# Clearing the substitution's result tiles and the HGRN queries' tiles on ScalarE in place of GpSimd

## The chip, the cores and the metric

The kernel runs on one core of a Trainium2 chip. The time is device microseconds (us) of one execution on that core. Its engines are called as in the profile: PE is TensorE, DVE is VectorE, ACT is ScalarE, POOL is GpSimd, SP is SyncE, which mostly issues DMAs. POOL issues DMAs of its own, too. Each engine runs its instructions in one fixed order and waits, by semaphores, for what other engines and DMAs deliver.

## What is computed

Two layers of a hybrid backbone for 512 latent tokens and a prefix of 256 context tokens, model width 1024, all in float32. Cut to what matters:

```python
for l in range(2):
    hl, hc = modulate(rmsnorm(xl), ...), modulate(rmsnorm(xc), ...)   # adaLN from c and c_ctx
    pl, pc = split_in(hl @ w_in[l]), split_in(hc @ w_in[l])           # one input projection
    dn = deltanet_group(...)   # gated delta rule, 4 heads of 64, chunks of 64, both directions
    sw = swa_group(...)        # 8 query heads, 2 kv heads, window 128, a sink, plus the context
    hg = hgrn2_group(...)      # HGRN2, 4 heads of 64, chunks of 64, both directions
    x = x + gate * (concat(dn, sw, hg) @ w_out[l])
    x = x + gate * (square(relu(modulate(rmsnorm(x)) @ w_ff1[l])) @ w_ff2[l])   # width 4096
return rmsnorm(xl)             # the context's stream is needed up to layer 1's projections
```

Two places of it bear on the change. The delta rule solves, for each chunk, a unit lower triangular system (`triangular_solve(a, rhs, unit_diagonal=True)`). The HGRN group forms masked products of queries and keys within a chunk.

## The kernel before, in words

**Products.** A float32 weight piece is split in two: L540 (ACT) casts it to `hi`, L541 (DVE) makes `lo`, and three matmuls, L554, L555 and L556, go over each tile of 128 rows. That is most of PE's work: input and output projections and the MLP, with L600 for the modulation vectors (adaLN).

**Stages of a layer.** The input projection fills tiles in SBUF and spills some of them to DRAM (`hq`, `hf`, `hi` for HGRN; `dg`, `hg` for the gates, L851). Then three groups run side by side. (1) Delta: `delta_prep` builds the chunk matrices (L1017 to L1041); `delta_inverse` calls `delta_blocks` for the substitution. That inverts blocks of 32 rows on DVE, in 31 pairs of a product (L1104) and an addition (L1105) of changing length; the result tile is `Yb`, cleared at L1092 with a diagonal of ones put in at L1093. Its blocks go through DRAM (`xu`, L1113, L1116, L1118) and are combined by small matmuls (L1135, L1139). `delta_chain` walks the chunks (L1177 to L1220) and `delta_norm` normalises (L1243 to L1257). (2) Attention: scores (L1450), softmax (L1475 and L1476 on DVE, L1480 and L1483 on ACT), products with the values (L1503, L1512). (3) HGRN: loads of `hf` and `hi` (L1273, L1282), two query tiles `qb`, cleared at L1299, of which the first then receives the queries by L1301; the second gets them times the forget products by L1315. Only the two blocks that belong to a head are written, the rest of the tile has to be zero, since L1309 and L1329 multiply the whole. Then the levels (L1329 and on), the chain of chunks (L1352 to L1395), and `head_norm` (L864 to L886). The output projection reads the three results (`yd`, `ys`, `yh`).

**What sets the order.** Each stage is a Python generator. `run(...)` (L274) advances several of them in turns, and `ahead(g, n)` gives the instructions of one a priority. A scheduler (`tile.TileContext(..., schedule_with_timeline_sim=True)`) then fixes the order of each engine from its own estimates of how long each instruction takes; so another engine for one instruction can change the order of many. In layer 0 the context's chain and HGRN run first (some 300 to 500 us), in layer 1 the three groups of the latent run together:

```python
run(self.ahead(delta(), 3000), self.ahead(att(), 1000), hg())
```

Here `att()` ends with the output projection's share of the attention (`ys`), whose products can stand between the steps of the other two.

**Memory.** SBUF is cut by hand: an arena and three regions r1, r2 and r3. Buffers are reused, so a clear waits for the last reader of what was there before. A tile of zeros of 128x256 exists (`self.zero`, L481, cleared once by DVE).

**Clears.** There are ten: `Yb` four times (64x1024 for the context, 128x1024 for the latent, in two layers) and the two `qb` three times (128x1024 for the context of layer 0, 128x2048 for the latent of either layer; the context of layer 1 needs no queries).

Of the kernel before, what the change touches and what calls it, by code (L numbers as in the profile page):

```python
# [167 lines left out]
def bc(ap, axis, n):  # L168
    ap = ap.unsqueeze(axis)
    return ap.broadcast_to(list(ap.shape[:axis]) + [n] + list(ap.shape[axis + 1:]))  # L170
# [99 lines left out]
def h4(ap):  # L270
    return ap.rearrange("p (h i) -> p h i", i=64)
# [33 lines left out]
class Net:  # L305
# [74 lines left out]
    def setup(self):  # L380
        nc = self.nc
# [66 lines left out]
        for l in range(DEPTH):  # L448
            if l:
                nc.vector.tensor_tensor(out=cum, in0=cum, in1=lb[:, :, :, l], op=ALU.add)  # L450
            v = self.lbn[:, l]
# [25 lines left out]
        st = self.keep(768)  # L477
        self.sd = st[:, 512:768]
        self.sh = st[:, 0:256].rearrange("p (a i) -> p a i", a=4)
        self.zero = st[:, 256:512].rearrange("p (a i) -> p a i", a=4)  # L480
        nc.vector.memset(self.zero, 0.0)  # L481
        kv = self.keep(2048)
        self.kT = kv[:, 0:1024]
        self.vS = kv[:, 1024:2048].rearrange("p (b c) -> p b c", b=8)
# [2 lines left out]
        self.ctx.kv0, self.lat.kv0 = 0, 512  # L487
        self.wh = Ring(self.wmem, 2, 1024)
        self.wl = Ring(self.wmem, 2, 1024)


    def x_load(self, seg, queue=None):
# [585 lines left out]
    def delta_blocks(self, seg):  # L1078
        nc, Uv = self.nc, seg.U
        n, u = 2 * seg.nc, slice(seg.u0, seg.u0 + 2 * seg.nc)  # L1080
        half, size = slice(4 * n, 8 * n), slice(0, 8 * n)
        Pb, Qb, Yb, tb = self.get(1024), self.get(1024), self.get(1024), self.get(256)
        P, Q, Y = (b.v.rearrange("p (a b) -> p a b", a=32) for b in (Pb, Qb, Yb))

        def quarters():

            for i in range(8):
                fw, hf, jb = i < 4, i // 2 % 2, i % 2
                rows = slice(64 * hf + 32 * jb, 64 * hf + 32 * jb + 32)
                yield slice(i * n, i * n + n), hf if fw else 1 - hf, rows, slice(32 * jb, 32 * jb + 32), fw, fw == (jb == 0)  # L1090

        nc.gpsimd.memset(Yb.v[size], 0.0)  # L1092
        nc.gpsimd.memset(Yb.v[size, 0:1024:33], 1.0)  # L1093

        nc.gpsimd.dma_start(out=seg.ud[:], in_=Uv[:, :, u])
        for blk, vv, rows, cols, fw, first in quarters():
            nc.gpsimd.dma_start(out=(P if fw else Q)[blk], in_=seg.ud[rows, vv, :, cols].rearrange("r u i -> u r i"))
        yield 8.0

        nc.vector.tensor_copy(P[half], Q[half].rearrange("p a b -> p b a"))  # L1100
        for c in range(31):
            m = 31 - c
            t = tb.v[size, :(c + 1) * m].rearrange("p (r m) -> p r m", m=m)
            nc.vector.tensor_tensor(out=t, in0=bc(Y[size, :c + 1, c], 2, m), in1=bc(P[size, c, c + 1:], 1, c + 1), op=ALU.mult)  # L1104
            nc.vector.tensor_tensor(out=Y[size, :c + 1, c + 1:], in0=Y[size, :c + 1, c + 1:], in1=t, op=ALU.subtract)  # L1105
            yield 0.3 + (c + 1) * m / 480
        Pb.free()
        tb.free()
        Z, Bb = Q, self.get(2 * n * 32)
        B = Bb.v.rearrange("p (v u i) -> p v u i", v=2, u=n)  # L1110
        nc.vector.tensor_copy(Z[size], Y[size].rearrange("p a b -> p b a"))
        for i, b in enumerate((Yb, Qb)):
            nc.gpsimd.dma_start(out=seg.xd[i], in_=b.v[size].rearrange("p (a b) -> p a b", a=32))  # L1113

        for blk, vv, rows, cols, fw, first in quarters():
            nc.gpsimd.dma_start(out=Uv[rows, vv, u, cols], in_=seg.xd[0 if fw else 1, blk].rearrange("u r i -> r u i"))  # L1116
            if first:
                nc.gpsimd.dma_start(out=B[rows, vv], in_=seg.xd[1 if fw else 0, blk].rearrange("u r i -> r u i"))  # L1118
        yield 10.0
        Qb.free()  # L1120
        Yb.free()
        Hr = Ring(self, 2, 512)
        for vv in range(2):
            firsts = []
            for hf in range(2):
                a, b = 64 * hf, 64 * hf + 32
                sa, sb = slice(0, 32), slice(32, 64)
                if hf != vv:
                    a, b, sa, sb = b, a, sb, sa
                firsts.append((slice(a, a + 32), slice(b, b + 32), sa, sb))  # L1130
            ph, pu, H = self.bank("ni"), self.bank("ni"), Hr()
            U = Uv[:, vv, u]
            for ra, rb, sa, sb in firsts:
                for k in range(n):
                    nc.tensor.matmul(ph[rb, k * 32:k * 32 + 32], lhsT=U[ra, k, sb], rhs=B[ra, vv, k], start=True, stop=True)  # L1135
                nc.scalar.copy(H[rb, :n * 32], ph[rb, :n * 32])
            for ra, rb, sa, sb in firsts:
                for k in range(n):
                    nc.tensor.matmul(pu[ra, k * 32:k * 32 + 32], lhsT=H[rb, k * 32:k * 32 + 32], rhs=U[rb, k, sb], start=True, stop=True)  # L1139
                nc.scalar.activation(out=U[ra, :, sb], in_=pu[ra, :n * 32].rearrange("p (u i) -> p u i", i=32), func=AF.Copy, scale=-1.0)  # L1140
            yield 2.0
        Bb.free()
        Hr.free()
# [123 lines left out]
    def hgrn(self, l, seg, need):  # L1267
        nc, T, nb, nC, r = self.nc, seg.T, seg.nb, seg.nc, seg.r
# [3 lines left out]
        for d in range(2):  # L1272
            nc.gpsimd.dma_start(out=kk[d], in_=seg.spill[l][d])  # L1273
            for p in range(2):
                a, na, b = (w[:, l, d, p:p + 1] for w in (self.lba, self.lbn, self.lbb))
# [5 lines left out]
        v = vb.v.rearrange("p (b c) -> p b c", b=nb)  # L1281
# [4 lines left out]
        def cells():  # L1286

            for n in range(2 * nb):
                for g in range(2):
                    t0 = n % nb * 128 + g * 64  # L1290
                    yield n, heads[g], n // nb, n // nb * nC + n % nb * 2 + g, slice(t0, t0 + 64)

        if need:

            qb = [self.get(4 * T) for _ in range(2)]
            qq = [b.v.rearrange("p (e x i) -> p e x i", e=2, i=64) for b in qb]
            qf = [[b.v[rows, e * 2 * T:e * 2 * T + 2 * T] for e, rows in enumerate(heads)] for b in qb]
            for b in qb:
                nc.gpsimd.memset(b.v, 0.0)  # L1299
            for e, rows in enumerate(heads):  # L1300
                nc.gpsimd.dma_start(out=qf[0][e].rearrange("p (a t) -> p a t", a=2), in_=seg.spill[l][2][rows])  # L1301

            scb = self.get(nb * 256)
            sc = scb.v.rearrange("p (n e i) -> p n e i", e=2, i=64)
            nc.vector.tensor_tensor(out=ks, in0=kk[0], in1=kk[1], op=ALU.add)
            for n, g, p, x, t in cells():
                if n % 4 == 0 and g is heads[0]:
                    ps = self.bank("hg")
                nc.tensor.matmul(ps[g, n % 4 * 128:n % 4 * 128 + 128], lhsT=ks[:, p, t], rhs=qq[0][:, :, x], start=True, stop=True)  # L1309
                if n % 4 == 3 and g is heads[1]:  # L1310
                    nc.vector.tensor_tensor(out=scb.v[:, (n - 3) * 128:(n + 1) * 128].rearrange("p (n i) -> p n i", i=64), in0=h4(ps),
                                            in1=bc(self.c["hd"], 1, 8), op=ALU.mult)
            for d in (1, 0):
                for e, rows in enumerate(heads):
                    nc.vector.tensor_tensor(out=qf[d][e], in0=qf[0][e], in1=F[d][rows].rearrange("p a t -> p (a t)"), op=ALU.mult)  # L1315
            yield T / 60
# [29 lines left out]
        for d in range(2):  # L1346
            for b0 in range(0, nb, 2):
                pt = self.bank("hg")
                for b in (b0, b0 + 1):
                    for p in range(2):  # L1350
                        c = (b - b0) * 256 + p * 128
# [24 lines left out]
        if need:  # L1376
# [13 lines left out]
            for c in range(nC):  # L1390
                g, b = c % 2, c // 2
# [364 lines left out]
```

## Time and profile before

| | |
|---|---|
| median of 3 runs | 2086.23 us (2084.28 to 2090.1) |
| profiled execution | 2089.67 us |
| span of its profile | 2087.8 us |
| mean granted clock of PE | 0.964 |
| PE busy | 1975.2 us (95%) |
| DVE busy | 1225.9 us (59%) |
| ACT busy | 860.6 us (41%) |
| POOL busy | 149.0 us (7%) |

Busy time is what an engine spends in instructions, its DMA issues, branches and semaphore waits aside. Matmuls overlap, so a busy PE is not a PE at its peak. The chain is followed back from the last instruction, at each step to what released it. Granted clock is the share of the full TensorE clock that the throttle gave, here 1.0 or about half. The profile's records are in the line numbers of the kernel before.

### The profile page before, as it was taken

What the parts mean: (1) busy time and instruction counts of PE and PEld (TensorE: products, weight loads), DVE (VectorE), ACT (ScalarE), POOL (GpSimd) and SP (SyncE); (2) the same over time, 40 slices, a digit from 0 to 9 for tenths busy, and PEclk for the clock granted to TensorE, in tenths of its full rate; (3) what the DMA queues carried; (4) which work ended last, traced back from release to release, by engine and by line L of the source; (5) the groups of instructions that cost most, each with busy time, mean ns of one, the idle gap of its engine ahead of it and who ended that gap; (6) DMA issues with size and microseconds to landing.
All of it is one profiled execution on the core that took longest, in us unless ns stands there. A gap on an engine that the chain in (4) does not pass through costs nothing.

```text
span 2087.8 us, 38082 instructions
## 1 busy us (share of the span) xinstructions
PE 1975.2 (95%) x15506; PEld 1627.2 (78%) x15506; DVE 1225.9 (59%) x2794; ACT 860.6 (41%) x1707; POOL 149.0 (7%) x289
## 2 busy tenths in 40 slices
PE   5999999899899999799999998999899979999996
PEld 3777888779899997788788875767678857888885
DVE  5675873756976676766333334756787573333335
ACT  3432354245556563452524232325544434334241
POOL 0001242000000000011000000012300000000000
PEclk9998997999999999899999999999989989999998
DMA  8545342165333342343222245364300222222222
GB/s 321 167 133 168 104 137 86 43 205 169 106 118 102 113 141 82 115 133 109 92 101 84 99 154 168 123 205 141 110 12 3 82 71 101 91 101 92 98 85 80
DMA packets 72831, 242.46 MB, mean 116 GB/s; under 512 B 10320, under 2 KB 13520, under 8 KB 72528
## 3 DMA queue, kind: packets, MB, share of 16 engines
q1 hardware_dynamic: 58608, 199.45, 28.4%
q0 software_dynamic: 12176, 35.19, 5.2%
q10 hardware_dynamic: 1872, 5.38, 0.8%
q8 instruction: 122, 2.00, 0.4%
q14 instruction: 53, 0.43, 0.1%
HBM read 218.21 MB, written 19.14 MB: 114 GB/s over the span
## 4 chain that ended last, share of the span: by engine, by line
PE 66%; issue 22%; DVE 5%; DMA 4%; ACT 2%; POOL 0%; SPq 0%; POOLq 0%; ACTq 0%; DVEq 0%
PE psum L554 15%; PE psum L556 15%; PE psum L555 14%; PE psum L600 3%; PE psum L1512 2%; PE psum L1503 2%; PE psum L1450 2%; DMA arena<-in_ada 1%; DMA r<-in_ada 1%; PE psum L1177 1%; PE psum L1329 1%; PE psum L1135 1%; PE psum L572 1%; PE psum L574 1%; PE psum L1139 1%
## 5 line engine op out<-in xcount | busy, mean ns | idle before, releaser
L554 PE MATMUL psum<-r,weights 128*128 128x512 f32 (+1 forms) x2288 | 823.9, 361 | 10.7 <-ACT arena L782 3.3
L556 PE MATMUL psum<-r,weights 128*128 128x512 f32 (+1 forms) x2288 | 819.8, 359 | 0.6 <-DVE weights L541 0.6
L555 PE MATMUL psum<-r,weights 128*128 128x512 f32 (+1 forms) x2288 | 818.7, 358 | 0.6 <-DVE r L1532 0.3
L540 ACT CAST weights<-arena 128x1024 fp32r<-128x1024 f32 (+3 forms) x295 | 293.6, 996 | 666.2 <-PE psum L555 583.7
L554 PEld LDWEIGHTS psum<-r,weights 128*128 128x128 f32 x2288 | 432.9, 189 | 96.1 <-issue 13.3
L541 DVE TENSOR_TENSOR weights<-arena,weights 128x1024 fp32r<-128x1024 f32 (+3 forms) x295 | 341.0, 1156 | 281.2 <-ACT weights L540 265.0
L556 PEld LDWEIGHTS psum<-r,weights 128*128 128x128 f32 x2288 | 432.6, 189 | 73.0 <-issue 4.4
L555 PEld LDWEIGHTS psum<-r,weights 128*128 128x128 f32 x2288 | 432.7, 189 | 69.2 <-issue 4.3
L1569 DVE SCALAR_TENSOR_TENSOR arena<-psum,arena 128x512 f32<-128x512 f32 (+1 forms) x94 | 61.9, 659 | 192.2 <-PE psum L556 191.9
L1556 DVE TENSOR_TENSOR r<-arena,r 128x512 fp32r<-128x512 f32 (+1 forms) x96 | 57.5, 601 | 36.1 <-ACT r L1555 35.8
L672 ACT ACTIVATE r<-arena 128x512 fp32r<-128x512 f32 (+1 forms) x56 | 33.0, 627 | 60.4 <-DVE arena L669 60.3
L1450 PE MATMUL psum<-r 128*128 128x256 f32 (+1 forms) x256 | 54.9, 327 | 0.2 <-ACT r L1483 0.2
L1554 ACT ACTIVATE arena<-arena 128x512 f32<-128x512 f32 (+1 forms) x96 | 53.9, 564 | 2.5
L1555 ACT CAST r<-arena 128x512 fp32r<-128x512 f32 (+1 forms) x96 | 52.6, 552 | 2.4
L1553 ACT ACTIVATE arena<-psum 128x512 f32<-128x512 f32 (+1 forms) x96 | 50.4, 525 | 0.0
L1540 DVE SCALAR_TENSOR_TENSOR arena<-psum,arena 128x512 f32<-128x512 f32 (+1 forms) x40 | 27.7, 695 | 34.8 <-PE psum L556 34.6
L572 PE MATMUL psum<-weights,r 128*128 128x400 f32 x96 | 35.9, 386 | 11.9 <-DVE arena L669 10.1
L600 PE MATMUL psum<-arena 128*32 128x256 f32 x448 | 40.0, 406 | 3.3 <-DMA arena<-in_ada 3.1
L1503 PE MATMUL psum<-arena,r 128*128 128x128 f32 x180 | 36.4, 291 | 7.0 <-ACT r L1480 6.3
L1508 ACT COPY arena<-psum 128x512 f32<-128x512 f32 x53 | 31.2, 590 | 25.8 <-PE psum L1503 25.4
L600 PE MATMUL psum<-r,arena 128*32 128x256 f32 x320 | 33.6, 461 | 7.5 <-DMA r<-in_ada 7.5
L1450 PEld LDWEIGHTS psum<-r 128*128 128x128 f32 x256 | 38.4, 198 | 2.7 <-issue 0.9
(455 smaller groups left out, 2638.3 us busy)
## 6 DMA issues: line engine op xcount, KB each, us to landing
arena<-in_ff SPq DMA_DIRECT2D x192, 512.0 KB, 3.2
arena<-in_ada SPq DMA_DIRECT2D x56, 512.0 KB, 4.6
arena<-in_win SPq DMA_DIRECT2D x51, 512.0 KB, 3.8
r<-in_ada SPq DMA_DIRECT2D x40, 512.0 KB, 5.3
arena<-in_wout SPq DMA_DIRECT2D x16, 512.0 KB, 3.2
arena<-in_win SPq DMA_DIRECT2D x12, 400.0 KB, 4.5
arena<-arena POOLq DMA_DIRECT2D x40, 64.0 KB, 4.4
arena<-in_x SPq DMA_DIRECT2D x4, 512.0 KB, 9.6
```

The lines of the kernel that those rows point to most:

```text
L540: nc.scalar.copy(hi, st)
L541: nc.vector.tensor_tensor(out=lo, in0=st, in1=hi.bitcast(F32), op=ALU.subtract)
L554: nc.tensor.matmul(o, lhsT=hi[:, w], rhs=h.hi(k), start=k == 0, stop=False)
L555: nc.tensor.matmul(o, lhsT=hi[:, w], rhs=h.lo(k), start=False, stop=False)
L556: nc.tensor.matmul(o, lhsT=lo[:, w], rhs=h.hi(k), start=False, stop=k == nk - 1)
L572: nc.tensor.matmul(ps[:, :w], lhsT=h.hi(k)[:, t], rhs=hi[:, c], start=k == 0, stop=False)
L600: nc.tensor.matmul(ps[32 * j:32 * j + 32, f * 256:f * 256 + 256], lhsT=self.csil[:, k, :], rhs=st[:, j * 256:j * 256 + 256], start=k == 0, ...
L1450: nc.tensor.matmul(o, lhsT=qs[:, kv], rhs=ks[:, kv, a, c0:c1], start=a == 0, stop=a == 1 and not more)
L1503: nc.tensor.transpose(pt[:, c:c + 128], Ps[kv][:, (k0 + kt) * 128:(k0 + kt) * 128 + 128], self.ident)
L1554: nc.scalar.activation(out=t, in_=t, func=AF.Square)
L1556: nc.vector.tensor_tensor(out=f.lo(k), in0=t, in1=f.hi(k).bitcast(F32), op=ALU.subtract)
L1569: nc.vector.scalar_tensor_tensor(out=seg.x[m], in0=ps, scalar=self.mod(l, 5, m, seg), in1=seg.x[m], op0=ALU.mult, op1=ALU.add)
```

## The change

The 128x256 tile of zeros gets a second, flat view, `self.zeros`. A new method `clear` views its argument as pieces of 256 columns and copies the zeros to all of them in one ACT instruction. The clears of L1092 and L1299 call it; the ten clears of POOL become ten COPYs of ACT. The diagonal of ones (L1093) stays on POOL and follows the clear, so that POOL waits for ACT there; the loads of L1301 do the same.

```diff
         self.zero = st[:, 256:512].rearrange("p (a i) -> p a i", a=4)
         nc.vector.memset(self.zero, 0.0)
+        self.zeros = st[:, 256:512]
...
+    def clear(self, v):
+
+        v = v.rearrange("p (n c) -> p n c", c=256)
+        self.nc.scalar.copy(v, bc(self.zeros[0:v.shape[0]], 1, v.shape[1]))
...
-        nc.gpsimd.memset(Yb.v[size], 0.0)
+        self.clear(Yb.v[size])
         nc.gpsimd.memset(Yb.v[size, 0:1024:33], 1.0)
...
             for b in qb:
-                nc.gpsimd.memset(b.v, 0.0)
+                self.clear(b.v)
```

Behind the new method every line stands six further down: L1480 of before is L1486 of after, L554 is L560. The prediction names the lines of before.

The order of the engines differs in two stretches of PE's order, about 300 to 500 us and 1270 to 1670 us of the trace of before; elsewhere PE's order is the same. Three places follow.

ACT, layer 1, at the attention's softmax, where the first query tile (in `r_13373`) is cleared. L849 evacuates a projection, L1496 and L1508 attention's sums, L1480 to L1483 are a softmax. Before:

```order
L1443 CAST r_12068<-arena 64x128 x2
L849 ACTIVATE arena<-psum 128x512
L1496 COPY arena<-psum 128x128
L1508 COPY r_11061<-psum 128x512
L1480 ACTIVATE r_11061,arena<-psum,arena 128x256
L1477 ACTIVATE arena<-arena 128x2
L1483 ACTIVATE r_11061,arena<-psum,arena 128x384
L1276 ACTIVATE r_13373<-r_13373,arena 128x512 x2
```

After:

```order
L1449 CAST r_12068<-arena 64x128 x2
L495 COPY r_13373<-arena 128x2048
L855 ACTIVATE arena<-psum 128x512
L1502 COPY arena<-psum 128x128
L1514 COPY arena<-psum 128x512
L1486 ACTIVATE r_11061,arena<-psum,arena 128x256
L1483 ACTIVATE arena<-arena 128x2
L1489 ACTIVATE r_11061,arena<-psum,arena 128x256
```

The clear, L495 of after, stands ahead of the evacuation of L855 (L849 before).

PE, layer 0, at the end of the context's chain and HGRN: L1352 and L1366 are HGRN's chunk products, L1257 the delta norm's transposes, L1210 the chain. Before:

```order
L1329 MATMUL psum<-arena,r_132 64x64 x16
L1352 MATMUL psum<-arena,r_132 128x128 x4
L1366 MATMUL psum<-arena 64x64 x16
L1352 MATMUL psum<-arena,r_132 128x128 x4
L1257 MATMUL psum<-arena 128x128 x4
L1366 MATMUL psum<-arena 64x64 x16
L1210 MATMUL psum<-arena 64x64
```

After, around the last of those L1366 (L1372 now; L560 to L562 are the matmuls of a product, here the context's output projection):

```order
L560 MATMUL psum<-r_128,weights 128x256
L561 MATMUL psum<-r_128,weights 128x256
L562 MATMUL psum<-r_128,weights 128x256
L1372 MATMUL psum<-arena 64x64 x16
L560 MATMUL psum<-r_128,weights 128x256
L561 MATMUL psum<-r_128,weights 128x256
L562 MATMUL psum<-r_128,weights 128x256
```

The output projection's products have moved to both sides of the HGRN step.

PE, layer 1, at the chain's end: L1218 and L1220 are its last step, L875 the head norm's sums, L1257 the delta norm's transposes, L886 the head norm's. Before, where L875 stands; 17 products are between the last L1220 and this, and 26 between the first of these rows of L875 and the first L1257:

```order
L556 MATMUL psum<-r_12068,weights 128x512
L875 MATMUL psum<-arena 128x2 x7
L554 MATMUL psum<-r_12068,weights 128x512
L555 MATMUL psum<-r_12068,weights 128x512
L875 MATMUL psum<-arena 128x2
L556 MATMUL psum<-r_12068,weights 128x512
L554 MATMUL psum<-r_12068,weights 128x512
L555 MATMUL psum<-r_12068,weights 128x512
```

After, from the last L1220 (L1226 now) on:

```order
L1226 MATMUL psum<-arena 64x64
L1224 MATMUL psum<-arena 64x64
L1226 MATMUL psum<-arena 64x64
L881 MATMUL psum<-arena 128x2 x8
L1263 MATMUL psum<-arena,r_11061 128x128 x4
L892 MATMUL psum<-arena 128x128 x8
L1263 MATMUL psum<-arena,r_11061 128x128 x2
L560 MATMUL psum<-r_12068,weights 128x512 x2
L1263 MATMUL psum<-arena,r_11061 128x128 x2
```

The products that stood between are earlier in the order of after, and L1226, L881 (L875 before), L1263 (L1257) and L892 (L886) follow one another.

## Rows read from the trace of the kernel before

**Rows 1.** The page: busy time of the engines, and the chain that ended last.

```profile
PE 1975.2 (95%) x15506; PEld 1627.2 (78%) x15506; DVE 1225.9 (59%) x2794; ACT 860.6 (41%) x1707; POOL 149.0 (7%) x289
...
PE 66%; issue 22%; DVE 5%; DMA 4%; ACT 2%; POOL 0%; SPq 0%; POOLq 0%; ACTq 0%; DVEq 0%
```

**Rows 2.** Groups by line, POOL: the clears; busy us, mean ns, idle before them.

```profile
L1299 POOL MEMSET arena<- 128x2048 f32 (+1 forms) x5 | 7.4, 1474 | 93.8 <-ACT r L1171 81.4 <-DVE arena L1191 10.3 <-DVE arena L1104 2.2
...
L1092 POOL MEMSET arena<- 128x1024 f32 (+1 forms) x3 | 3.3, 1116 | 67.7 <-DVE r L1532 46.2 <-ACT r L672 18.5 <-PE psum L1013 3.0
...
L1299 POOL MEMSET r<- 128x2048 f32 x1 | 1.8, 1824 | 0.0
...
L1092 POOL MEMSET r<- 64x1024 f32 x1 | 1.0, 951 | 2.9 <-DVE arena L860 2.9
```

**Rows 3.** Line L1299: who waited for its clears (us, times).

```profile
  POOL arena L1301: 0.3, 1
```

**Rows 4.** Groups by line and form, ACT: weight casts; busy us, mean ns.

```profile
L540 ACT CAST weights<-arena 128x1024 fp32r<-128x1024 f32 x259 | 272.0, 1050 | 607.2 <-PE psum L555 560.0 <-DMA arena<-in_ff 16.7 <-issue 13.5
...
L540 ACT CAST weights<-arena 128x512 fp32r<-128x512 f32 x8 | 4.9, 619 | 11.2 <-PE psum L555 7.5 <-issue 2.5 <-DMA arena<-in_wout 1.2
```

**Rows 5.** Timeline, POOL, layer 1: start us, duration us.

```profile
1486.83 1.82 POOL L1299 MEMSET r<- 128x2048 f32 x1
```

**Rows 6.** Timeline, DVE, the same moment.

```profile
1486.38 2.30 DVE L1475 TENSOR_SCALAR arena<-arena 128x2 f32<-128x2 f32 x1
1486.44 2.23 DVE L1476 TENSOR_TENSOR arena<-arena 128x2 f32<-128x2 f32 x1
1486.52 2.16 DVE L1105 TENSOR_TENSOR arena<-arena,r 128x175 f32<-128x175 f32 x1
```

**Rows 7.** Line L1475, 1440 to 1560 us: duration ns min/median/max.

```profile
L1475 DVE TENSOR_SCALAR arena<-arena x10: 159/169/2301, 1441.5 to 1555.9; 128x2 f32<-128x2 f32 x10
```

**Rows 8.** Timeline, ACT and PE, after that: idle before and its releaser in brackets.

```profile
1488.71 0.47 ACT L1480 ACTIVATE r<-psum,arena 128x256 f32<-128x256 f32 x1 [4.18 <-DVE arena L1105]
...
1489.33 0.47 PE L1503 MATMUL psum<-arena,r 128*128 128x128 f32 x1 [4.08 <-ACT r L1480]
```

**Rows 9.** Layer 1 stretches: length, busy PE, PEld, DVE, ACT, POOL, clock, DMA, GB/s.

```profile
1486.00:1490.00 4.00, 0.49 (x2) 0.20 (x2) 3.82 (x10) 1.29 (x6) 3.94 (x5) 0.79 0.94 323
1490.00:1494.00 4.00, 3.39 (x13) 2.54 (x13) 3.32 (x15) 4.00 (x9) 0.61 (x2) 0.50 0.63 176
1494.00:1498.00 4.00, 1.75 (x11) 1.18 (x12) 3.02 (x9) 3.92 (x9) 1.87 (x4) 0.86 0.66 262
```

**Rows 10.** The same, layer 0: end of the context's chain.

```profile
380.00:390.00 10.00, 7.02 (x131) 5.86 (x130) 9.76 (x35) 2.67 (x7) 0.00 (x0) 0.96 0.01 2
390.00:400.00 10.00, 6.98 (x134) 6.34 (x135) 8.71 (x39) 2.25 (x5) 0.00 (x0) 0.53 0.15 53
400.00:410.00 10.00, 9.99 (x196) 9.64 (x194) 3.20 (x15) 2.13 (x5) 0.00 (x0) 1.00 0.17 57
```

**Rows 11.** Timeline, PE, layer 1: the chain's last step and the norm behind it.

```profile
1650.77 0.33 PE L1220 MATMUL psum<-arena 64*64 64x64 f32 x4
...
1662.74 0.38 PE L1257 MATMUL psum<-arena,r 128*128 128x128 f32 x2
```

**Rows 12.** Timeline, DVE and ACT, the same norm.

```profile
1651.13 1.06 ACT L871 ACTIVATE arena<-arena 128x1024 f32<-128x1024 f32 x1 [1.85 <-PE psum L1220]
1652.10 1.04 ACT L1243 ACTIVATE r<-arena 128x1024 f32<-128x1024 f32 x1
...
1653.18 1.22 DVE L1245 TENSOR_REDUCE arena<-r 128x16 f32<-128x1024 f32 x1
...
1658.93 1.22 DVE L1249 TENSOR_TENSOR r<-arena 128x1024 f32<-128x1024 f32 x1
```

**Rows 13.** The same, layer 1: the chain's end.

```profile
1560.00:1627.00 67.00, 64.04 (x1251) 55.93 (x1250) 50.32 (x168) 34.61 (x108) 0.00 (x0) 1.00 0.01 3
1645.00:1668.00 23.00, 22.65 (x161) 18.97 (x157) 16.84 (x49) 5.58 (x9) 0.00 (x0) 1.00 0.23 79
```

## The prediction

> **What bounds the kernel now.** I read the page first. TensorE (PE) is busy for 95% of the span and holds two thirds of the chain that ended last; ScalarE (ACT) is busy 41%, GpSimd (POOL) 7% [rows 1]. So nothing that POOL or ACT does counts by itself. It counts where PE stands still behind it, or where the granted clock falls after PE stood still. Then I read the groups by line for the cleared tiles [rows 2], who waited for them [rows 3], the timelines around the one clear that has a visible victim [rows 5, 6, 8], the busy time by stretches where PE has gaps [rows 9, 10, 13], and the order of before against that of after. The reader is to see that the clears themselves wait on other engines for far longer than they run, that one of them falls on a VectorE (DVE) stall, and that the stages touched lie at about 300 to 500 us (layer 0) and 1270 to 1670 us (layer 1). Outside these PE runs the same order in both kernels.
>
> **What is taken off POOL.** Ten clears: 7.4 + 3.3 + 1.8 + 1.0 = 13.5 us [rows 2]. The only wait that the trace puts down to a line of them is 0.3 us of POOL itself, at L1301 [rows 3]. Work off the path, therefore worth nothing directly.
>
> **What is put on ACT.** No row of before shows ACT copying zeros, so I bound it by its weight casts of the same shapes: 1.05 us for 128x1024 and 0.62 for 128x512 [rows 4], hence about 0.43 us more for each 512 columns, and 1.05 + 2 x 0.43 = 1.91 us for 128x2048 (an estimate). Six clears of 1024 columns and four of 2048 come to 6 x 1.05 + 4 x 1.91 = 13.9 us, much what POOL needed. ACT is in order, so each clear delays what is queued behind it. In the order of after the eight early ones stand between steps with ACT idle around them (casts of weights which wait 560 of 607 idle us for PE to release a buffer [rows 4]); cover: that idle time. The two of layer 1 stand in the attention, where ACT is busy for 4.00 and 3.92 us of 4 [rows 9]. The first goes ahead of L849, L1496 and L1508 into the 4.18 us in which ACT idles [rows 8] and fits; the second stands directly before an L1480 that PE's L1503 waits for. Ends: 0 (both hidden) and 2 x 1.91 = 3.8 us (neither). I take **+1**, nearer to hidden, because the first has a measured gap.
>
> **What is moved: the stall at 1486 us.** Three DVE instructions begin at 1486.38, 1486.44 and 1486.52, last 2.30, 2.23 and 2.16 us and so end together at 1488.68 [rows 6]; the line of the first has a median of 0.169 us [rows 7]. A POOL clear of 1.82 us runs from 1486.83 to 1488.65 [rows 5]. [...] What is late next is ACT: it is full from 1490 to 1498 [rows 9], so a faster clock there would mostly make PE wait longer; of the 3.39 PE-busy us at half clock I give back a quarter, 0.9. Together **-3**, with ends 0 (another GpSimd instruction, a DMA issue, meets the same DVE step) and -5.5 (2.1 and both halves of the 3.39 twice over, 1.7 + 1.7).
>
> [...]
>
> **What is moved: layer 0, 300 to 500 us.** At the end of the context's chain DVE is busy 9.76 and 8.71 us of 10 and PE only 7.0 and 7.0; the granted clock is 0.53 from 390 to 400 [rows 10]. In the order of after, products of the context's output projection (L554 to L556, 128x256) stand before and behind the last L1366, where before has none; from 400 on PE is full [rows 10], so what is done earlier shortens the rest. At best the gap of 3.0 + 3.0 us closes and the half clock goes with it (I allow 2 of the 4.7 us which a full 10 us at 0.53 would lose): -8. At worst the products sit in front of hgrn steps that DVE already waits for, about 5 us of PE work, which one gap of this sort buys back in part: +4. I take **-3**, half the gap.
>
> **What is moved: layer 1, 1270 to 1670 us.** The scheduler's order puts the delta stream later: counted in matmuls at their durations in the trace (an estimate), its last L1210 stands some 16 us of PE work further on, the attention's last steps some 7 us earlier. What this costs is read at the chain's end. Before, from its last L1220 at 1650.77 to the first L1257 at 1662.74 [rows 11], 12.0 us pass, and products of the attention's share of the output projection (L554 to L556) cover them: PE is busy 22.65 of 23 us [rows 13]. In after L1220, L875, L1257 and L886 stand in a row with nothing between. The norm's latency is then bare: L1243 1.04, L1245 1.22, about eleven small DVE steps of 0.17 (1.9), L1249 1.22, and 0.4 for the chain's last addition make 5.8 us; with L871's 1.06 ahead on ACT 6.9 [rows 7, 12]. The products are not lost, they stand some 15 us of work earlier; but between 1560 and 1627 PE has only 3.0 idle us that they could fill [rows 13], and they went into the chain's last steps, which were covered before too. So 6 to 7 us less 1 to 2: **+5**. Upper end +10: the 6.9, and a clock that falls after them as it did after 4.08 us, 3.39 us of work at 0.50 [rows 9] costing 1.7 in one such stretch and the same again in a second. Lower end -4: the mixture of attention with the chain's inverse fills as much as 1486 to 1498 shows idle at PE (3.5 + 0.6 + 2.3 = 6.4 us [rows 9]), over the part that the stall already counts (2.1).
>
> **Sum.** Against the profiled execution, 2089.67 us: +1 - 3 - 3 + 5 = 0. That execution is 3.44 above the median of the three, so I forecast 2086.2, rounded **2086 us**.
>
> **Rivals.**
> The gaps close (faster). Both moved stages go well: the collision with its clock -5.5, layer 0 -8, layer 1 at 0 and the clears hidden: -13.5, 2073. For it: DVE-bound gaps at 380 to 400 with fill put right there. Against: the bare norm. With each at half of this, 2079; I price it between, at 2077. Chance 0.27.
> The chain's end is bare (slower). Layer 1 at +10, the collision -2.1, layer 0 at 0, clears +2: +10, 2096. It decides if PE idles for over 6 us between the last L1220 and the first L1257 and no stretch before 1627 gains. For it: the order, and 12.0 us of cover now. Against: the same products fill something else. Chance 0.24.
> The clears hold up ACT (slower). A clear in front of a waiting weight cast or softmax: four of 1.91 and the rest hidden is 7.6, with the other terms at -1 some 2093. Against: 560 idle us before the casts. Chance 0.05.
> The collision was everywhere. If every clear held DVE for its whole length, 13.5 us of DVE come free, and were each on the path, 2072.7. Against: rows 3, and only this one clear has an ending in common with a DVE stall that PE waited for. Chance 0.03. [...]
>
> **How the numbers follow.** My forecast, terms that cancel to within the bound of 0.3% (6.3 us, about what a measurement of this kernel can tell from no change), has 0.41. Faster: 0.27 + 0.03 = 0.30. Slower: 0.24 + 0.05 = 0.29. The ends added up give -17.5 and +17.8; not all meet, so I cut each side to where a tenth is left: 2073 to 2100.
>
> **What would show it.** Right or wrong by step: ten COPYs on ACT of about 1.05 and 1.9 us, none followed by an idle PE; no DVE L1475 over 0.3 us and a first gap of about 2 us, not 4.08, before that softmax's L1503; PE idle at 380 to 400 below 4 us; PE idle 5 to 7 us between the last L1220 and the first L1257, which now is covered. The forecast fails if that last idle time is under 2 us (then faster), or if the attention or the chain's inverse ahead of it stands still for more than now (then slower).

## The result

The change made the kernel slower: 2105.88 us against 2086.02 us (medians of four runs each), a ratio of 1.009 with a 95% interval of 1.0069 to 1.0112, or 20 us. I had forecast 2086 us, 2073 to 2100. Ratios, here and below, are of undisturbed executions; one execution of a later kernel (GpSimd, end bare) took 4761.44 us and is not in its ratio.

The profiled execution has a span of 2104.7 us, 16.9 more than before's. That this is less than 20 lies in the executions that were profiled: before's is 3.65 us above its median of four, the changed kernel's 0.61. The page of the changed kernel, busy time by engine and instructions, beside [rows 1]:

```profile
span 2104.7 us, 38066 instructions
## 1 busy us (share of the span) xinstructions
PE 1980.8 (94%) x15506; PEld 1626.5 (77%) x15506; DVE 1226.3 (58%) x2794; ACT 874.7 (42%) x1717; POOL 134.9 (6%) x279
...
PE 65%; issue 23%; DVE 5%; DMA 3%; ACT 2%; POOL 0%; SPq 0%; POOLq 0%; ACTq 0%; DVEq 0%
```

POOL lost 14.1 us of work and ACT gained 14.1, as the change says. Nothing else in this table moves by 20 us (PE's busy time, for the same 15506 matmuls, by 5.6), and the table cannot say where the time went. Matching each matmul of the changed trace with its counterpart in the trace before does: the offset between them is +1.4 us at 200 to 300 us (the two executions already differ by that at 60 us, long before any clear), +0.3 after layer 0's context stage at 500 us, -1.8 from 860 to 1270 us, and +16.9 from 1700 us to the end. So in this pair of traces layer 0's stretch brought 1.2 us back, another 2.1 came between 500 and 860 us, where both kernels run one order, and the stretch of layer 1 from 1270 to 1690 us cost 18.6. All that has to be explained is in the last.

There, the delta stream's last preparation matmul and the norms' last matmul stand as follows. The lines are those of the two kernels by line and engine (shortest, median and longest in ns, then first and last start in us); L1047 and L892 are L1041 and L886 of before. Before:

```profile
L1041 PE MATMUL psum<-arena x64: 269/269/321, 1391.4 to 1430.6; 64*64 64x128 f32 x64
L886 PE MATMUL psum<-arena x16: 274/275/275, 1665.5 to 1667.2; 128*128 128x128 f32 x16
```

After:

```profile
L1047 PE MATMUL psum<-arena x64: 268/269/321, 1388.6 to 1442.4; 64*64 64x128 f32 x64
L892 PE MATMUL psum<-arena x16: 420/422/583, 1680.5 to 1683.8; 128*128 128x128 f32 x16
```

From the last L1041 to the last L886 before took 236.6 us, after 241.4. The end of the stage is 16.6 us later, and 11.8 of that is already there at 1442 us, when the delta preparation ends: before the substitution has begun, and before a single query tile of this layer is cleared.

PE's order is the same in both kernels up to a matmul at 1290.0 us before and 1288.3 after. From there to the last L886, with the same matmuls in another order, the rows of the two traces are (length, busy PE, PEld, DVE, ACT, POOL, clock, DMA, GB/s), before and after:

```profile
1290.00:1667.20 377.20, 358.44 (x3715) 286.08 (x3715) 260.54 (x698) 164.99 (x408) 42.92 (x78) 0.96 0.31 100
1288.30:1683.80 395.50, 364.52 (x3714) 288.08 (x3713) 260.80 (x699) 170.27 (x411) 38.25 (x75) 0.94 0.30 95
```

Of the 18.3 us 12.2 are idle PE (31.0 us, 18.8 before), and 6.1 are PE busy for longer, at a mean granted clock of 0.94 where it was 0.96. Of the idle time 3.6 us come up to the last L1041, 2.4 from there to the last L1220 (L1226 after), and 6.2 behind it.

What PE waited for, in the stretch 1380 to 1697 us after (sum, times, longest):

```profile
PE psum L606 <- DMA arena<-in_ada: 4.8, 4, 3.4
PE psum L1518 <- ACT arena L1502: 4.2, 2, 2.2
PE psum L1263 <- DVE arena L525: 4.1, 1, 4.1
PE psum L1335 <- DVE arena L1346: 3.5, 3, 2.3
PE psum L1509 <- ACT r L1486: 2.4, 1, 2.4
```

The last is the softmax's wait, whose longest was 4.08 us [rows 8]: the stall is gone. The third is the bare norm at the chain's end that the prediction named. The first is adaLN's matmuls (L606, L600 before), which the scheduler now issues sooner and whose weights are not there; before, the same wait was 2.0 us. No wait of PE names a clear (L495), but the second names L1502 (L1496 before), an ACT copy that stands behind a clear; more on this below.

### The profile page after: what moved, and what is told of

It is laid out like the page before. It is cut to its first block, busy times and chain, and to the rows that moved or that the text cites. A ratio compares the mean times of both kernels' runs of the same rounds, so it can differ in the third digit from the quotient of the medians.

```text
span 2104.7 us, 38066 instructions
## 1 busy us (share of the span) xinstructions
PE 1980.8 (94%) x15506; PEld 1626.5 (77%) x15506; DVE 1226.3 (58%) x2794; ACT 874.7 (42%) x1717; POOL 134.9 (6%) x279
## 4 chain that ended last, share of the span: by engine, by line
PE 65%; issue 23%; DVE 5%; DMA 3%; ACT 2%; POOL 0%; SPq 0%; POOLq 0%; ACTq 0%; DVEq 0%
PE psum L560 15%; PE psum L562 15%; PE psum L561 14%; PE psum L606 3%; PE psum L1518 2%; PE psum L1509 1%; PE psum L1456 1%; DMA r<-in_ada 1%; PE psum L578 1%; DMA arena<-in_ada 1%; PE psum L1183 1%; PE psum L579 1%; PE psum L580 1%; PE psum L1335 1%; PE psum L1145 1%
## 5 line engine op out<-in xcount | busy, mean ns | idle before, releaser
L560 PE MATMUL psum<-r,weights 128*128 128x512 f32 (+1 forms) x2288 | 824.6, 361 | 11.0 <-ACT arena L788 3.2
L562 PE MATMUL psum<-r,weights 128*128 128x512 f32 (+1 forms) x2288 | 819.9, 359 | 1.1 <-DVE weights L547 1.0
L560 PEld LDWEIGHTS psum<-r,weights 128*128 128x128 f32 x2288 | 432.3, 189 | 96.6 <-issue 12.8
L562 PEld LDWEIGHTS psum<-r,weights 128*128 128x128 f32 x2288 | 432.3, 189 | 73.8 <-issue 5.2
L606 PE MATMUL psum<-arena 128*32 128x256 f32 x448 | 40.3, 405 | 5.7 <-DMA arena<-in_ada 5.7
L1514 ACT COPY arena<-psum 128x512 f32<-128x512 f32 x53 | 31.2, 590 | 25.5 <-PE psum L1509 25.1
L606 PE MATMUL psum<-r,arena 128*32 128x256 f32 x320 | 34.0, 469 | 7.6 <-DMA r<-in_ada 7.6
```

Source lines behind the costliest of these rows:

```text
L560: nc.tensor.matmul(o, lhsT=hi[:, w], rhs=h.hi(k), start=k == 0, stop=False)
L562: nc.tensor.matmul(o, lhsT=lo[:, w], rhs=h.hi(k), start=False, stop=k == nk - 1)
L606: nc.tensor.matmul(ps[32 * j:32 * j + 32, f * 256:f * 256 + 256], lhsT=self.csil[:, k, :], rhs=st[:, j * 256:j * 256 + 256], start=k == 0, ...
```

## The experiments

Since the diff changes the scheduler's order as well as the engines, the question is which of the two costs. A clear can be given to ScalarE one by one; the order of TensorE's instructions that results was compared with those of before and after for each choice, and the choices that keep one thing and alter the other were run. In these kernels `clear` takes a key for each call (`Y` result tile, `Q` query tile; `c` context, `l` latent; layer; `a`, `b` the two query tiles):

```diff
...
+        if key + str(n) + which not in self.ON_ACT:
+            self.nc.gpsimd.memset(v, 0.0)
+            return
         v = v.rearrange("p (n c) -> p n c", c=256)
         self.nc.scalar.copy(v, bc(self.zeros[0:v.shape[0]], 1, v.shape[1]))
```

**Six clears, with the order of before.**

```diff
+    ON_ACT = ('Yc0', 'Yl0', 'Yc1', 'Yl1', 'Ql0a', 'Ql0b')
```

> Six of the ten clears on ScalarE: the four result tiles of the substitution and the two latent query tiles of layer 0. TensorE's order is that of the kernel before but for 4 neighbouring matmuls near 500 us. Theory 'order' (the engine of a clear costs nothing, the rearranged order of layer 1 costs everything): 2086 us, within 4 of before. Rival 'ScalarE' (each clear delays what is queued behind it by about the 2 us per clear that 20 us over ten clears come to): 6 x 2 = +12, 2098 us.

Measured: 2087.77 us, ratio 0.9996 (0.9979 to 1.0013). Six of ten clears on ScalarE cost nothing that shows (by the interval 2.7 us at most). The rival would have had 12 us.

This kernel keeps the layer 1 query clears on POOL, and in it the collision of [rows 5, 6] comes again, to a tenth of a microsecond. Its timeline of POOL and DVE (L500 is the POOL clear, L1489, L1490 and L1119 are L1475, L1476 and L1105 of before):

```profile
1482.53 1.82 POOL L500 MEMSET r<- 128x2048 f32 x1
...
1482.06 2.32 DVE L1489 TENSOR_SCALAR arena<-arena 128x2 f32<-128x2 f32 x1
1482.13 2.25 DVE L1490 TENSOR_TENSOR arena<-arena 128x2 f32<-128x2 f32 x1
1482.20 2.18 DVE L1119 TENSOR_TENSOR arena<-arena,r 128x175 f32<-128x175 f32 x1
```

**Three clears, all of layer 0.**

```diff
+    ON_ACT = ('Yc0', 'Qc0a', 'Qc0b')
```

> Three clears on ScalarE: the context's of layer 0 (result tile and two query tiles). Every clear of layer 1 stays on GpSimd. TensorE's order becomes that of the changed kernel up to 500 us, and in layer 1 the delta preparation comes late as in the changed kernel (last L1041 about 9 us of TensorE work later), but 32 products still stand between the chain's last L1220 and the first L1257 (43 before, none in the changed kernel). Theory 'order': slower without one moved clear in layer 1: half of the loss from the late preparation and its waits, 2092 to 2097 us. Rival 'bare end' (only the missing cover at the chain's end costs): 2085 to 2088. Rival 'ScalarE': 3 x 2 = +6, all of it before 500 us.

Measured: 2103.67 us, ratio 1.0097 (1.0063 to 1.0132). Three clears before 400 us, with every clear of layer 1 where it was, cost as much as all ten. They cost it a thousand microseconds later: in this trace the delta preparation ends at 1446.7 us (1430.6 before) and the norms' last matmul is at 1679.7 (1667.2).

```profile
L1055 PE MATMUL psum<-arena x64: 269/269/320, 1393.2 to 1446.7; 64*64 64x128 f32 x64
L900 PE MATMUL psum<-arena x16: 275/275/377, 1678.0 to 1679.7; 128*128 128x128 f32 x16
```

Theory and both rivals missed by size: I expected at most 2097. But 'ScalarE' has nothing to put in layer 1, and 'bare end' nothing with 32 products left there, so the order is what remains; I had undervalued the late preparation.

**The two clears in the attention.**

```diff
+    ON_ACT = ('Ql1a', 'Ql1b')
```

> Two clears on ScalarE: the latent query tiles of layer 1, the ones that fall in the attention. TensorE's order is that of before up to about 1450 us, and 43 products still stand between the last L1220 and the first L1257. Theory 'order': no loss, and the stall of VectorE at 1486 us is gone: 2082 to 2087 us. Rival 'ScalarE': these two are the clears in the busiest stretch of ScalarE, +4 to +10, 2090 to 2096.

Measured: 2089.0 us, ratio 1.0011 (0.9994 to 1.0028). No loss, but no gain either. The stall is gone, as the line of L1475 (here L1489) shows first in this kernel, then in the one above which keeps the POOL clear:

```profile
L1489 DVE TENSOR_SCALAR arena<-arena x10: 153/165/177, 1443.8 to 1555.7; 128x2 f32<-128x2 f32 x10
```

```profile
L1489 DVE TENSOR_SCALAR arena<-arena x10: 160/169/2320, 1437.2 to 1550.7; 128x2 f32<-128x2 f32 x10
```

What came in its place is seen in the same kernel's ACT timeline and PE's waits: the clear itself, 1.90 us, and other steps of the attention that PE waits for.

```profile
1485.57 1.90 ACT L503 COPY r<-arena 128x2048 f32<-128x2048 f32 x1 [0.36 <-PE psum L570]
...
1487.87 0.26 ACT L1510 COPY arena<-psum 128x128 f32<-128x128 f32 x1
```

```profile
1488.18 0.66 PE L1526 MATMUL psum<-arena 128*64 128x128 f32 x8 [1.98 <-ACT arena L1510]
```

```profile
PE psum L1526 <- ACT arena L1510: 3.1, 2, 2.0
PE psum L1517 <- ACT arena L1522: 3.0, 2, 2.3
```

The copy L1510 (L1496 before) stands behind the clear in ACT's order, and PE stands still for 1.98 us until it has come: about as long as the stall of 2.1 us that is gone.

**The query tiles alone.**

```diff
+    ON_ACT = ('Qc0a', 'Qc0b', 'Ql0a', 'Ql0b', 'Ql1a', 'Ql1b')
```

> The six query tiles on ScalarE, the four result tiles on GpSimd as before. TensorE's order is exactly that of the changed kernel. Theory 'order': the changed kernel's time, 2106 us within 4. Rival 'ScalarE': four clears of ten taken back, -8, 2098.

Measured: 2107.46 us, ratio 1.0097 (1.0061 to 1.0133): the changed kernel's loss with four clears taken back. Same order (but for two neighbouring matmuls near 407 us), same time.

The next kernels alter one number of the schedule and leave the clears alone.

**Ten clears on ScalarE, preparation early.**

```diff
-        run(self.ahead(prep(1, (lat,)), 3000), self.project_swa(1, (lat,)), ada(1, 2))
+        run(self.ahead(prep(1, (lat,)), 3000), (self.project_swa(1, (lat,)), 0.7), ada(1, 2))
```

> The changed kernel with all ten clears on ScalarE and one number altered: the window attention's projection of layer 1 is advanced at 0.7 of its rate beside the delta preparation, which puts the last L1041 back to 128.5 us of TensorE work after a common point (130.1 before, 139.4 in the changed kernel), and 36 products stand between the last L1220 and the first L1257. Theory 'delta path' (the last L1041 starts a path of constant length, some 235 to 240 us, to the end of the norms): 2085 to 2091 us, the whole loss back. Rival 'ScalarE in layer 1': 2100 or more, since the clears are where they were.

Measured: 2091.19 us, ratio 1.0012 (0.9997 to 1.0028). Nearly all of the loss is back with all ten clears on ScalarE; the time is at the upper end of what I expected.

**Ten clears on ScalarE, preparation late, the end covered.**

```diff
-        run(self.ahead(prep(1, (lat,)), 3000), self.project_swa(1, (lat,)), ada(1, 2))
+        run(self.ahead(prep(1, (lat,)), 3000), self.project_swa(1, (lat,)), (ada(1, 2), 0.8))
```

> The changed kernel with another number altered: adaLN of layer 1 advanced at 0.8 of its rate in the same stage. The last L1041 stays at 139.4 us of TensorE work, but 32 products are back between the last L1220 and the first L1257 (none in the changed kernel). Theory 'delta path': 2100 to 2106 us, the cover gives back nothing or little. Rival 'bare end' (the missing cover is what costs): 2088 to 2094.

Measured: 2102.39 us, ratio 1.0066 (1.0046 to 1.0086), 14 us over before in the same session, though the cover at the chain's end is back. 'Bare end' alone falls.

**Clears on GpSimd, the end bare.** The kernel before, with

```diff
-        run(self.project_dn(1, (lat,)), ada(1, 1))
+        run(self.project_dn(1, (lat,)), (ada(1, 1), 0.8))
```

> The kernel before, all clears on GpSimd, with adaLN of layer 1 advanced at 0.8 of its rate beside the delta projection: the last L1041 is early (128.5), but not one product stands between the last L1220 and the first L1257, as in the changed kernel. Theory 'delta path': 2086 to 2092 us, since the path starts as early as before. Rival 'bare end': 2096 to 2102.

Measured: 2093.79 us against 2088.66, ratio 1.0026 (1.001 to 1.0042): 5 us. That is between the two forecasts. The bare end has a price, about what my prediction gave it, and is not the 20 us.

**Clears on GpSimd, preparation late.** The kernel before, with

```diff
-        run(self.ahead(prep(1, (lat,)), 3000), self.project_swa(1, (lat,)), ada(1, 2))
+        run(self.ahead(prep(1, (lat,)), 0), self.project_swa(1, (lat,)), ada(1, 2))
```

> The kernel before, all clears on GpSimd, with the delta preparation's priority of 3000 taken away in layer 1: the last L1041 falls to 139.6 us of TensorE work, as late as in the changed kernel; 10 products are left at the chain's end. Theory 'delta path': 2098 to 2106 us without any clear moved. Rival 'ScalarE': 2086, no loss where no clear is moved. Rival 'bare end': 2092 to 2096.

Measured: 2095.35 us, ratio 1.0028 (1.0016 to 1.0041). Slower without a clear moved, as 'ScalarE' cannot have it; but 7 us, less than I expected, and inside what I had given 'bare end'. By itself this run does not choose between the two.

**Two more orders.** The first is the changed kernel with

```diff
-        run(self.ahead(prep(1, (lat,)), 3000), self.project_swa(1, (lat,)), ada(1, 2))
+        run(self.ahead(prep(1, (lat,)), 3000), self.project_swa(1, (lat,)), (ada(1, 2), 0.5))
```

> The changed kernel, all ten clears on ScalarE, with adaLN of layer 1 advanced at half its rate beside the delta preparation: last L1041 at 128.8 us of TensorE work (130.1 before, 139.4 in the changed kernel), 51 products between the last L1220 and the first L1257 (43 before). Theory 'the later of two': the end is set by the delta path where that starts late, and by TensorE's own work where it starts early, so that an earlier start gains nothing: 2084 to 2091 us. Rival 'delta path alone': 2080 to 2084, as the path starts some 2 us earlier than before and has more cover.

Measured: 2095.18 us, ratio 1.0051 (1.0031 to 1.0071). Missed by 4 us. Here the preparation ends as early as before, and the time is lost at the other end: 51 products now stand between the last L1220 and the first L1257, and from the last L1220 to the last L886 24.0 us pass (16.3 before, 13.1 in the changed kernel).

The second is the kernel before with the 0.7 of above.

> The kernel before, all clears on GpSimd, with the window attention's projection advanced at 0.7 of its rate, as in the run with the early preparation and the clears on ScalarE: last L1041 at 128.5 us of TensorE work, 45 products at the chain's end. Theory 'the later of two': 2084 to 2091 us, and within 4 us of the kernel with the same number and the clears on ScalarE. Rival 'ScalarE': faster than that one by more than 4 us. Rival 'delta path alone': 2080 to 2084.

Measured: 2076.43 us, ratio 0.996 (0.9936 to 0.9984), faster than both kernels. Both parts of the theory missed: an early start did gain, and the kernel with the same number and the clears on ScalarE is, by the ratios (1.0012 and 0.996), 11 us slower. Is that ScalarE after all? In the traces the two are level when the chain of chunks begins (first L1177 at 703.0 us after a common point with the clears on ScalarE, 702.7 on GpSimd), which is after the last clear; they part behind it, in a different order of the products. The last two runs hold the order fixed:

> The same kernel as the run with the early preparation and all clears on GpSimd, measured in five rounds, beside the next one. If its gain is real: 2074 to 2081 us, ratio 0.994 to 0.998. If it was chance of the first measurement: 2084 to 2089.

> The same, with six of the ten clears on ScalarE (result tiles of both layers, latent query tiles of layer 0); TensorE's order is that of the kernel with the early preparation and all clears on GpSimd, but for 4 neighbouring matmuls near 500 us. Theory 'order': the same time as that kernel, within 3 us. Rival 'ScalarE': up to 2 us for each of six clears, +6 to +12.

Measured: 2075.97 us, ratio 0.9949 (0.993 to 0.9968), and with six clears on ScalarE 2076.37 us, ratio 0.994 (0.9916 to 0.9964). The gain is real, some 12 us; with the order held, the engine of six clears is again worth nothing. No run holds this order with all ten on ScalarE, so that the 11 us of the kernel with ten come from its order is argued from where the two traces part.

**All together.** The start is the last L1041, counted from a matmul at about 830 us (all of these run one order from 505 to about 1290 us); the path is from there to the last L886; the end is the sum. These come from one trace of each kernel, the ratios from all its runs. The two traces of one and the same kernel (GpSimd, preparation early, and again) are 2.3 us apart at the end, so differences of that size say nothing.

| kernel | clears on ACT | start | path | end | ratio |
|---|---|---|---|---|---|
| six, preparation early | 6 | 598.3 | 229.5 | 827.8 | 0.994 |
| GpSimd, preparation early | 0 | 596.3 | 231.3 | 827.6 | 0.996 |
| the same, again | 0 | 597.4 | 232.5 | 829.9 | 0.9949 |
| ten, preparation early | 10 | 594.8 | 239.6 | 834.4 | 1.0012 |
| six, order of before | 6 | 600.2 | 235.5 | 835.8 | 0.9996 |
| two in the attention | 2 | 600.0 | 236.4 | 836.3 | 1.0011 |
| GpSimd, end bare | 0 | 598.6 | 238.3 | 836.9 | 1.0026 |
| before | 0 | 600.6 | 236.5 | 837.1 | 1 |
| ten, adaLN at half | 10 | 600.6 | 241.3 | 841.9 | 1.0051 |
| GpSimd, preparation late | 0 | 608.2 | 235.7 | 843.9 | 1.0028 |
| ten, preparation late | 10 | 608.9 | 238.2 | 847.1 | 1.0066 |
| three of layer 0 | 3 | 614.2 | 233.1 | 847.2 | 1.0097 |
| six query tiles | 6 | 611.7 | 241.0 | 852.7 | 1.0097 |
| the change | 10 | 612.8 | 241.5 | 854.3 | 1.009 |

The starts differ by 19 us, the paths by 12, and no column of clears orders the ratios: six clears are at the top and near the bottom. From the end to the start of PE's last matmul 411.7 to 414.5 us follow in every one of these traces (412.1 before, 412.3 in the changed kernel), so the end of this stage is the time, but for what comes ahead of the common point. Five kernels start more than 7 us late, and all five end late, with and without the clears moved. The end followed when the start of the delta path was moved on purpose (late on GpSimd, early and late on ScalarE). Each of these kernels rearranges other products of the stage with it, so a start moved by itself was not measured. That the path's length is constant is not so: it varies by 6 us to either side with the order inside it, and for kernels which start early that is what decides.

## Why the prediction was wrong, point by point

**ScalarE's price: the durations right, the cover wrong.** Ten COPYs, of 1.05 us and 1.90 us; I had estimated 1.05 and 1.91. ACT's busy time rose by 14.1 us (estimate 13.9). The groups of the clear in the changed kernel, the arena's and the region's:

```profile
L495 ACT COPY arena<-arena x8: 1042/1050/1908, 236.4 to 1510.8; 128x1024 f32<-128x1024 f32 x4, 128x2048 f32<-128x2048 f32 x3, 64x1024 f32<-64x1024 f32 x1
...
L495 ACT COPY r<-arena x2: 1054/1476/1899, 226.2 to 1482.5; 64x1024 f32<-64x1024 f32 x1, 128x2048 f32<-128x2048 f32 x1
```

For six of the clears no price shows (0.9996). For the first one in the attention it does: I had it fit into 4.18 us in which ACT idles, ahead of L1496. In the changed kernel the input of that copy (L1502 there), a matmul of L1501, starts at 1482.27 us and lasts 0.38; the clear goes ahead of the copy, and PE stands still for 1.98 us:

```profile
1482.46 1.90 ACT L495 COPY r<-arena 128x2048 f32<-128x2048 f32 x1 [1.00 <-PE psum L562]
...
1484.76 0.26 ACT L1502 COPY arena<-psum 128x128 f32<-128x128 f32 x1
```

```profile
1485.07 0.66 PE L1518 MATMUL psum<-r,arena 128*64 128x128 f32 x8 [1.98 <-ACT arena L1502]
```

The kernel with only the two clears of the attention on ScalarE has the same wait, of 1.98 us. So the price there is about 2 us, not the +1 for everything.

**The stall at 1486 us: the collision right, its worth wrong.** In the changed kernel L1475 (L1481 there) takes 169 ns at the longest:

```profile
L1481 DVE TENSOR_SCALAR arena<-arena x10: 156/162/169, 1454.4 to 1546.3; 128x2 f32<-128x2 f32 x10
```

The kernel with six clears, where the POOL clear is still in layer 1, has the same stall of 2.32 us, ending 0.03 us after the clear. So the stall is in these two traces, which have this clear on POOL (2.30 and 2.32 us), and not in the changed kernel's. Another trace shows which instructions a clear held. With the preparation late and the clears on GpSimd, a clear runs from 1515.92 to 1517.74 us: the two-input L1474 and the copy out of PSUM, L1506, keep their usual 0.16 and 0.42 us inside it, and L1475, which has one input, in SBUF, takes 0.56 us in place of 0.17 and ends 0.03 us after the clear:

```profile
1515.92 1.82 POOL L1299 MEMSET arena<- 128x2048 f32 x1
...
1516.79 0.16 DVE L1474 SCALAR_TENSOR_TENSOR arena<-arena 128x2 f32<-128x2 f32 x1
1516.87 0.42 DVE L1506 COPY r<-psum 128x256 f32<-128x256 f32 x1
1517.21 0.56 DVE L1475 TENSOR_SCALAR arena<-arena 128x2 f32<-128x2 f32 x1
```

As the two-input L1474 keeps its length there, the two instructions that end with L1475 in [rows 6], which have two inputs, fit as waiting behind it in DVE's order (my reading, not tested), and the collision was not everywhere. But I credited 3 us: 2.1 for the stall, its 2.30 us [rows 6] less the usual 0.17 [rows 7], and 0.9 for the granted clock. No run shows the 0.9: from 1490 to 1500 us the mean granted clock is 0.67 before and 0.66 in the changed kernel. And the two clears moved alone gave none of the 3 us (1.0011, at best 1.3 us by its interval). The 2.1 us of DVE are gone, and the 1.98 us that PE waits behind the clear on ACT have come in their place.

**Layer 0: the gap filled, a gain not shown.** PE's busy time at the end of the context's chain rose, beside [rows 10]:

```profile
380.00:390.00 10.00, 7.73 (x104) 6.41 (x100) 9.70 (x35) 1.08 (x3) 0.00 (x0) 0.69 0.08 28
390.00:400.00 10.00, 8.80 (x182) 7.82 (x182) 7.76 (x28) 3.48 (x8) 0.00 (x0) 0.97 0.09 30
```

2.5 us of the 6.0 idle us were filled between these times, and 1.2 us arrived at 500 us, for which I had put 3. The other traces do not bear even this out: from the matmul at 300 us of before to that at 505 the six kernels with this order of layer 0 take 203.4 to 208.6 us, the eight with that of before 202.4 to 207.1.

**Layer 1: the step that failed.** I put +5 there, -4 to +10, and it was +18.6 with the stall's gain in it. I had seen the delta stream fall back, and wrote that its last L1210 stands 16 us of PE work further on. Then I asked what that uncovers at the chain's end, as if the order mattered only for what fills PE's gaps. The sum is that of another question: when does this stream end? Its preparation ended 12.2 us later by the common point at 830 us, and 13.5 us later counted from the matmul at 1290 us, shortly before the orders part: 9.9 us of more busy PE ahead of it (9.3 by the order at the trace's durations, which could be read beforehand) and 3.6 us of more idle PE, of which 2.8 are adaLN's matmuls waiting for their weights (4.8 against 2.0). The rest of the stream took 236.5 us before and takes 241.5 here (229.5 to 241.5 in all the traces). The term I should have written is the lateness of the last L1041, 9 to 13 us, and beside it the change in the path's length, which was +5.0 and which nothing that I read beforehand gave.

The bare end that I did price came as described. After the last L1226 (L1220 before) PE stands still for the head norm, and then for the delta norm:

```profile
1670.62 0.33 PE L1226 MATMUL psum<-arena 64*64 64x64 f32 x4
...
1672.15 1.95 PE L881 MATMUL psum<-arena 128*128 128x2 f32 x16 [1.20 <-ACT arena L877]
...
1678.21 0.66 PE L1263 MATMUL psum<-arena,r 128*128 128x128 f32 x2 [4.11 <-DVE arena L525]
```

```profile
1670.00:1680.00 10.00, 3.92 (x52) 3.26 (x48) 7.49 (x31) 2.01 (x2) 0.00 (x0) 0.70 0.00 0
1680.00:1690.00 10.00, 8.74 (x34) 5.95 (x32) 7.98 (x17) 3.09 (x6) 0.00 (x0) 0.79 0.00 0
```

PE is idle for 6.1 of the 10 us behind 1670 (I had said 5 to 7), and the granted clock falls to 0.70 and 0.79 (0.50 in each us from 1675 to 1684), where before it was 1.00 [rows 13]. Yet from the last L1220 to the last L886 it now takes 13.1 us, not 16.3: without products in between the norm itself is quicker. A bare end costs since the products were spent earlier, on gaps that the delta path did not need filled. Alone it measured 5 us (1.0026). The sign that I had named for a slower kernel came as well: between the last L1041 and the last L1220 PE stands still for 17.2 us, 14.8 before.

**The range and the rivals.** The rival 'chain's end bare' had the right sign and place and a price of +10; its condition on idle PE came true (6.2 us there), but it decided by the wrong point (idle PE at the end) and lacked the start of the stream. 'The clears hold up ACT' has one wait of 1.98 us for it, at the attention's first clear, and nothing else in any run.

**What stays open.** In the six kernels that have the changed order of layer 0's context stage, and in that with clears on GpSimd and the end bare, the medians are some 3 to 6 us above what the end of the layer 1 stage gives (ten, preparation early: -2.7 at the end, +2.5 in the median). Most of this can lie in which executions were profiled: that of before is 3.65 us above its median in the result, those of the others lie from 5.1 below to 8.5 above theirs. One trace of each kernel does not place the rest. That PE's longer busy time in the stage of layer 1 (6.1 us, at the lower clock) follows from its idle time there was not tested. Nor did a run show why the scheduler's order in layer 1 depends on three clears of layer 0; that it does is seen in the order alone.

## What to carry to other kernels

Where a scheduler orders the instructions, moving a microsecond of idle work to another engine is not a local edit: compare the orders of every later stage, and for the stream with the longest chain of dependences ask first when its last input is ready, and only then what fills the gaps. A stall that a trace shows plainly is worth only what its stage gives back; here 2.1 us of stall on VectorE went, and TensorE waited 1.98 us behind the same clear on ScalarE instead. An idle gap on the new engine is cover only if nothing that others wait for is queued behind the work that is put there. And the order can be had without the edit: one rate in one call (0.7 for the attention's projection) was worth 12 us, more than any engine for the clears.

## What the runs showed of the hardware

ScalarE copies zeros to 128x1024 in 1.05 us and to 128x2048 in 1.90 us, much like GpSimd's 1.82 for the latter [rows 5]; for a 64x1024 tile it needs as long as for 128x1024 (1.054 us for that in a region). In two kernels a VectorE instruction on 128x2 elements (L1475, 0.17 us by its median) began 0.45 and 0.47 us ahead of a GpSimd clear, while POOL issued a DMA, and ended 0.03 us after the clear, 2.30 and 2.32 us long; in the layer 1 attention of the two kernels shown without that clear no L1475 takes over 0.18 us (0.169 and 0.177 at the longest). The longest L1475 of four more traces with the query clears on GpSimd takes 1.29 us (three of layer 0), 0.56 (preparation late, shown beside its clear above), 0.38 (preparation early, again) and 0.37 (six, preparation early). One COPY, usually of 0.22 us, started 0.25 us into a clear, took 1.66 and ended 0.08 us after the clear:

```profile
1507.27 1.83 POOL L1299 MEMSET arena<- 128x2048 f32 x1
```

```profile
1507.52 1.66 DVE L1490 COPY arena<-arena 128x128 f32<-128x128 f32 x1
```

Beside the second query clear of the attention in the trace of before (1504.96 to 1506.78 us) VectorE's instructions keep their length: L1470 and L1469, which read PSUM, take 0.69 and 0.55 us, and L1514, L1445 and L1472, which have two inputs, 0.28, 0.29 and 0.16 (0.68, 0.56, 0.28, 0.29 and 0.15 from 1482 to 1486 us, ahead of the first). The clear itself can be the longer one: in the trace of before L1092's of 64x1024 takes 0.95 us at 224.86 us and 1.44 us at 765.06, where DVE's COPY L882 of 128x1024 had begun 0.14 us ahead of it; that the copy is the cause was not tested.
